# Normalising the softmax weights while they are split into halves, with four places for the halves, in a hybrid RG-LRU / forgetting-attention trunk on Trainium2

## The chip, the core and the metric

The kernel runs on one core of a Trainium2 chip. The metric is device time in microseconds (us) of one execution. A core has five engines that work side by side and meet through semaphores: PE multiplies matrices, DVE (VectorE) and ACT (ScalarE) do elementwise work and reductions, POOL (GpSimd) does slower elementwise work and issues some DMAs, and SP issues the rest of the DMAs. Every engine takes its instructions strictly in its own order: an instruction that waits holds back all that stand behind it on that engine.

## The reference, cut to what matters

Two layers: an RG-LRU layer, then forgetting attention (FoX) with 16 heads of 64 over 1024 positions, then a final norm. The change lies in the attention layer.

```python
def fox_mixer(h, w_in, b_f, w_out):
    u = h @ w_in
    q, k, v, gate = ...                       # (1, 1024, 16, 64) each, gate (1, 1024, 1024)
    cum = jnp.cumsum(jax.nn.log_sigmoid(f_logit), axis=1)
    ...
    logits = jnp.einsum("bqhd,bkhd->bhqk", q_blk, kf) * scale
    logits = logits + (cq_blk[..., :, None] - ck[:, :, None, :])
    logits = jnp.where(mask[None, None], logits, NEG_INF)
    p = jax.nn.softmax(logits, axis=-1)
    o = jnp.einsum("bhqk,bkhd->bqhd", p, vf)
    ...
    y = o * jax.nn.silu(gate)
    return y @ w_out
```

## The kernel before

Float32 products are made of halves: an operand is split into a high part and a low part (`to_hi`, `to_lo`, lines 88 to 102), and three products of parts are summed. The first 440 us hold the RG-LRU layer, which the change leaves as it is. The attention layer follows.

**One block of softmax** (`maxima`, line 718). A head's 1024 queries are taken in 8 blocks of 128 (i = 0 to 7); block i has (i+1)·128 keys. For each block: PE makes the logits S in PSUM (two places for S); DVE adds the mask and takes the row's maximum m in one custom instruction (line 742); ACT takes the exponential p and the row's sum (line 747); ACT writes the high half of p, times a constant, as float16 (line 752, booked on line 93); DVE writes the low half (line 753); one DMA issued by SP turns both halves over (`pT`, line 754), since the next product needs the keys on the partitions. There are two places for p, and two for the pair of halves, called `pp`. A place of `pp` is free again when its transposing DMA has landed. Below, "high half" and "low half" mean the two instructions that fill `pp`.

**The weighted values** (`weigh`, line 784). PE multiplies v with `pT` into O (PSUM) for half a head's queries, c = 0 (blocks 0 to 3) or c = 1 (blocks 4 to 7). ACT copies one part of O to `yo`, DVE adds the other (lines 804 and 805).

**The row sums.** Softmax divides by them. At the end of a head the 8 sums are scaled and inverted on DVE (lines 763 and 764), turned by PE (`tr`, line 766), copied (`rc`), written to DRAM and read back as a broadcast over 64 partitions by two DMAs on POOL's queue (`recd`, `recb`, lines 769 and 773). POOL multiplies the gate `sg` by them (`scale`, line 782), and then `yo` by the gate (`gated`, line 814). For heads up to 12 `yo` then goes to DRAM (`y1d`, line 820).

**The values of four heads** (`values`, line 541, and `bound`, line 524). Heads 0, 4, 8 and 12 begin with new v. 192 products `vps` make 8 tiles of 128 positions, 24 products each. Four tiles have room in PSUM: the 97th product needs the first tile to be read out. The read-out needs a factor: ACT squares the 8 weight tiles (`sqw`, two places), PE sums each over its rows (`norms`), DVE takes the maximum, ACT a square root, DVE a reciprocal and the factors `rv`; then ACT and DVE read the tiles out (lines 583 and 584).

**The order.** The text `ORDER` (line 29, and `LAST` for heads 12 to 15) says how PE's products are woven: a 0 or 1 is a step of `weigh` or `maxima`, a point is a step of six products of the projections around it (the next pair's q, k and gate; at the end the output product). From this a scheduler that simulates the engines fixes the order of every engine at build time. SP and POOL queues are in order as well; an issue on SP waits until the DMA eight issues earlier has landed. At the end, sums `xp` of the output are written to DRAM by POOL's queue (`x1d`, line 891) and read back by SP.

Of the kernel before, what the change touches and what calls it, by code (L numbers as in the profile page):

```python
# [23 lines left out]
NB = 12  # L24
HEADS = 16
HD = 64
# [14 lines left out]
def trunk(ctx: ExitStack, tc: tile.TileContext, xt, w0, wg, wo0, pc, gn, gf, w1, wv, wf, bf, wo1, out):  # L41
    nc = tc.nc

    def pool(name, bufs, **kw):
        return tc.tile_pool(name=name, bufs=bufs, **kw)

    const = ctx.enter_context(pool("const", 1))
    dram = ctx.enter_context(pool("dram", 1, space=DRAM))
    hpool = ctx.enter_context(pool("hT", 16))
    wpool = ctx.enter_context(pool("w", 4))  # L50
    ps = ctx.enter_context(pool("ps", 2, space=PSUM))
# [12 lines left out]
    ident = const.tile([P, P], F32, name="ident")  # L64
# [16 lines left out]

    pct = const.tile([P, 8, NB], F32, name="pct")
    gnt = const.tile([P, 2, KT], F32, name="gnt")
    cw = [pct[:, j] for j in range(4)]
    cb, ba, bx, ap_ = (pct[:, j] for j in range(4, 8))

# [102 lines left out]
    with ExitStack() as l0:  # L189
        xpool = l0.enter_context(pool("x", 1))  # L190
        ypool = l0.enter_context(pool("y", 2 * GROUP))
        lru = l0.enter_context(ExitStack())
# [9 lines left out]

        sm = const
        c2 = sm.tile([P, NB], F32, name="c2")
# [290 lines left out]
    cumd = dram.tile([HEADS, 2, SEQ], F32, name="cumd")  # L495
    recd = dram.tile([HEADS, 8, P], F32, name="recd")

    with ExitStack() as l1:
# [25 lines left out]
        def bound(g, parts):  # L524

            row = ps.tile([P, HALF], F32, tag="O", name="norms")[:, :256]
            for k in range(KT):
                sq = at.tile([P, 256], BF16, tag="sqw", name="sqw", bufs=2)
                nc.scalar.activation(sq, f32(parts[k][0][:, :256]), AF.Square, scale=gnt[:, 1, k : k + 1])
# [3 lines left out]
            nc.scalar.activation(most, most, AF.Sqrt, bias=tiny, scale=SEQ / TOP / TOP)  # L533
            nc.vector.reciprocal(most, most)
# [56 lines left out]
        sgs = {}  # L591
        recs = {}
        yos = {}
# [55 lines left out]

        fz = const.tile([P, 8, HEADS], F32, name="fz")  # L650
        Vs = {}
        bft = const.tile([HEADS, 1], F32, name="bft")
        nc.sync.dma_start(bft, bf)
        unit = at.tile([HEADS, HALF], F32, tag="recb", name="unit", bufs=1)
        nc.gpsimd.memset(unit, 1.0)
        cum = at.tile([HEADS, SEQ], F32, tag="sg", name="cum")

        def forget(half):
            cs = slice(half * HALF, (half + 1) * HALF)
            pt = ps.tile([P, HALF], F32, tag="O", name="fps")  # L660
            for i in range(4):
                if half and i > 1:
                    yield
                with tc.issue_after(pe[0].ins):
                    transpose(pt[:HEADS, i * P : (i + 1) * P], fz[:, half * 4 + i], ident)
            z_, e_ = (at.tile([HEADS, HALF], F32, tag=t, name=n, bufs=2) for t, n in (("p", "z"), ("pp", "e")))
            parts = [at.tile([HEADS, HALF], F32R, tag="yo", name="cp", bufs=2) for i in (3, 4)]
# [50 lines left out]
        def maxima(hd, c):  # L718
# [7 lines left out]
            for i in range(4 * c, 4 * c + 4):  # L726
# [26 lines left out]
                nc.vector.scalar_tensor_tensor(both[:, :, 1], p, TOP, both[:, :, 0], ALU.mult, ALU.subtract)  # L753
                nc.sync.dma_start_transpose(
# [3 lines left out]
                yield  # L758
            if hd == HEADS - 1 or c == 1:
                b0, b1 = (4 * c if hd == HEADS - 1 else 0), 4 * c + 4  # L760
                nb = b1 - b0
                sums = sums[:, b0:b1]
                nc.vector.tensor_scalar(sums, sums, tops[hd // 4], 2.0 * TOP, ALU.mult, ALU.mult)
                nc.vector.reciprocal(sums, sums)
                tr = ps.tile([P, P], F32, tag="O", name="tr")
                nc.tensor.transpose(tr[:nb], sums, ident)
                rc = at.tile([8, P], F32, tag="rc", name="rc", bufs=1)
                nc.vector.tensor_copy(rc[:nb], tr[:nb])
                nc.gpsimd.dma_start(recd[hd, b0:b1], rc[:nb])
                if s == 0:  # L770
                    recs[pair] = at.tile([P, SEQ], F32, tag="recb", name="recb", bufs=1)
                rows = slice(s * HD, (s + 1) * HD)
                nc.gpsimd.dma_start(
                    recs[pair][rows, b0 * P : b1 * P],
                    recd[hd : hd + 1, b0:b1].rearrange("o b q -> o (b q)").to_broadcast([HD, nb * P]),
                )
                yield

        def scale(hd, cs=slice(0, SEQ)):
            rows = slice((hd % 2) * HD, (hd % 2 + 1) * HD)  # L780
            sg = sgs[hd // 2][rows, cs]
            nc.gpsimd.tensor_tensor(sg, sg, recs[hd // 2][rows, cs], ALU.mult)

        def weigh(hd, c, sub=slice(0, HALF)):
# [18 lines left out]
            r0, r1 = s * HD, (1 - s) * HD  # L803
            nc.scalar.copy(yo[r0 : r0 + HD], O[r1 : r1 + HD])
            nc.vector.tensor_tensor(yo[r0 : r0 + HD], yo[r0 : r0 + HD], O[r0 : r0 + HD], ALU.add)
            yield

        def gated(hd, c, sub=slice(0, HALF)):

            if hd % 2 == 0:  # L810
                return
            pair = hd // 2
            yo = yos[pair, c][:, sub]
            nc.gpsimd.tensor_tensor(
                yo, yo, sgs[pair][:, c * HALF + sub.start : c * HALF + sub.stop], ALU.mult
            )
            if hd == 15:
                split_y(c, pair, yo, sub)
            elif hd < 13:
                nc.sync.dma_start(y1d[c, pair], yo)  # L820
# [90 lines left out]
        def turned(c, q):  # L911
# [11 lines left out]
            for b in range(2):  # L923
# [4 lines left out]
                for h, (d0, nd) in enumerate(parts):  # L928
# [6 lines left out]
                    for k in range(2):  # L935
# [5 lines left out]
                        if k == 0:  # L941
                            yield
                    sq = at.tile([P, HALF], F32, tag="pp", name="sq1", bufs=2)[:, : nd * P]
                    nc.scalar.activation(sq, pt, AF.Square, accum_out=ss[:, min(h, ss.shape[1] - 1)].unsqueeze(1))
# [59 lines left out]
        for hd in range(HEADS):  # L1004
# [28 lines left out]
            scale(hd)  # L1033
            gated(hd, 0)
# [17 lines left out]
        quarters = [slice(0, 256), slice(256, HALF)]  # L1052
        scale(15, slice(0, HALF))
# [4 lines left out]
        scale(15, slice(HALF, SEQ))  # L1058
        gated(15, 1, quarters[0])
# [76 lines left out]
```

## Time and profile before

| what | value |
|---|---|
| time, median of 3 runs | 1126.28 us (1125.81 to 1129.25) |
| the profiled execution's own time | 1126.19 us |
| its span, first to last instruction | 1124.4 us |
| PE busy | 1067.5 us (95% of the span) |
| DVE, ACT, POOL busy | 760.9, 611.2, 195.1 us |
| mean granted PE clock | 0.989 of full |

The profiled execution agrees with the median to 0.1 us, so its rows can be used for the sum directly. In the page's rows a time is in us, a group shows its count, busy time and mean duration in ns, and "idle before" is the time for which the engine stood still ahead of an instruction, with what ended it. A row of waits reads: engine, tile and line that waited, what it waited for, total us, number, longest. In rows by stage the columns are from:to, length, busy us of PE, of PE's weight loads, of DVE, ACT and POOL (with counts), granted PE clock, DMA share and GB/s.

### The profile page before, as it was taken

To read this page: it belongs to the slowest core of one execution; us is meant where nothing else is said; L and a number is where in the kernel's file an instruction comes from. 1 tells how busy PE (TensorE), PEld (TensorE's weight loads), DVE (VectorE), ACT (ScalarE), POOL (GpSimd) and SP (SyncE) were. 2 spreads that over 40 slices of the span, in tenths; PEclk is the share of its full clock that TensorE was granted. 3 is DMA by queue.
4 is the path that set the end of the run, shared out by engine and by line. 5 is a ranking of instruction groups with operands and counts; after the bars stand their busy time and mean duration, and the time that the engine had idled before them with its cause. 6 is when DMAs were issued, how large, how long until landed. Compare 5 with 4: busy or idle time off the path is not lost.

```text
span 1124.4 us, 14773 instructions
## 1 busy us (share of the span) xinstructions
PE 1067.5 (95%) x5147; PEld 850.3 (76%) x5147; DVE 760.9 (68%) x1216; ACT 611.2 (54%) x1053; POOL 195.1 (17%) x155
## 2 busy tenths in 40 slices
PE   9999999999999999899998999998999999989987
PEld 7788888888888887787666787667866678767666
DVE  7888755776568789547766557675567655677645
ACT  8488345355453656456555555565555555454434
POOL 1322212221121201420121201212012120112220
PEclk9999999999999999989998999999999999999999
DMA  6111111111111114417898938997398982999795
GB/s 236 57 47 43 52 52 52 38 58 45 53 38 52 47 44 144 130 56 164 176 192 161 181 81 177 192 181 177 87 177 185 164 179 73 227 229 220 195 244 187
DMA packets 214450, 143.13 MB, mean 127 GB/s; under 512 B 161348, under 2 KB 176324, under 8 KB 214376
## 3 DMA queue, kind: packets, MB, share of 16 engines
q1 hardware_dynamic: 211256, 133.73, 50.6%
q0 software_dynamic: 3120, 8.46, 2.6%
q8 instruction: 41, 0.67, 0.3%
q14 instruction: 33, 0.27, 0.1%
HBM read 63.30 MB, written 15.93 MB: 70 GB/s over the span
## 4 chain that ended last, share of the span: by engine, by line
PE 63%; DMA 17%; DVE 10%; ACT 5%; issue 3%; SPq 1%; POOL 0%; ACTq 0%; DVEq 0%; POOLq 0%
PE gps L56 19%; PE ops L56 13%; DMA pT<-pp 13%; PE ups L56 12%; PE vps L56 8%; PE gate L56 3%; DVE pp L753 3%; PE turn L56 3%; PE O L56 2%; ACT pp L93 2%; DVE S L742 2%; PE S L56 2%; DMA wf<-in_wo 1%; ACT p L747 1%; DVE wl L102 1%
## 5 line engine op out<-in xcount | busy, mean ns | idle before, releaser
L56 PE MATMUL gps<-hh,wh 128*128 128x512 f32 x576 | 234.9, 408 | 0.7 <-DVE qkl L621 0.7
L56 PE MATMUL gps<-hl,wh 128*128 128x512 f32 x576 | 228.2, 396 | 0.0
L56 PE MATMUL gps<-hh,wl 128*128 128x512 f32 x576 | 227.5, 395 | 0.0
L753 DVE SCALAR_TENSOR_TENSOR pp<-p,pp 128x128 f16<-128x128 f32 (+7 forms) x128 | 111.1, 868 | 118.4 <-ACT pp L93 117.5
L102 POOL TENSOR_TENSOR wl<-wf,wh 128x512 fp32r<-128x512 f32 (+1 forms) x60 | 100.8, 1685 | 397.5 <-ACT wh L91 359.9
L91 ACT CAST wh<-wf 128x512 fp32r<-128x512 f32 (+2 forms) x156 | 93.5, 603 | 112.3 <-PE ops L56 47.8
L93 ACT ACTIVATE pp<-p 128x128 f16<-128x128 f32 (+7 forms) x128 | 87.4, 684 | 113.8 <-DMA pT<-pp 112.4
L56 PEld LDWEIGHTS gps<-hl,wh 128*128 128x128 f32 x576 | 109.0, 189 | 25.9 <-issue 0.5
L56 PEld LDWEIGHTS gps<-hh,wh 128*128 128x128 f32 x576 | 109.6, 190 | 23.9 <-DVE qkl L621 0.9
L56 PE MATMUL S<-T,U 96*128 96x512 f32 (+7 forms) x384 | 98.7, 367 | 28.1 <-ACT p L747 28.1
L56 PEld LDWEIGHTS gps<-hh,wl 128*128 128x128 f32 x576 | 109.6, 190 | 20.1
L747 ACT ACTIVATE p<-S,m 128x128 f32<-128x128 f32 (+7 forms) x128 | 94.3, 737 | 51.1 <-DVE m L742 49.6
L56 PEld LDWEIGHTS S<-T,U 128*128 128x128 f32 (+1 forms) x384 | 68.5, 195 | 51.3 <-ACT p L747 39.4
L742 DVE CUSTOM_DVE_ANT_0 S<-S,mask 128x128 f32<-128x128 f32 (+7 forms) x128 | 96.6, 757 | 8.7 <-PE S L56 7.0
L387 DVE TENSOR_TENSOR x<-x,ops 128x512 f32<-128x512 f32 x80 | 54.1, 682 | 47.6 <-PE ops L56 47.6
L56 PE MATMUL O<-pT,v 128*128 128x512 f16 (+3 forms) x396 | 77.8, 324 | 4.0 <-DMA pT<-pp 1.8
L56 PE MATMUL vps<-wh,hh 128*128 128x256 f32 (+1 forms) x256 | 74.5, 291 | 7.3 <-DVE v L584 4.0
L102 DVE TENSOR_TENSOR wl<-wf,wh 128x512 fp32r<-128x512 f32 x96 | 68.1, 712 | 16.6 <-ACT wh L91 16.4
L56 PE MATMUL ups<-hh,wh 128*128 128x512 f32 x192 | 76.2, 398 | 0.9 <-ACT hh L93 0.9
L56 PE MATMUL ups<-hl,wh 128*128 128x512 f32 x192 | 76.6, 399 | 0.0
L56 PE MATMUL ops<-yh,wh 128*128 128x512 f32 x192 | 76.0, 396 | 0.5 <-DVE x L480 0.5
L56 PE MATMUL ups<-hh,wl 128*128 128x512 f32 x192 | 76.3, 397 | 0.0
(190 smaller groups left out, 2043.5 us busy)
## 6 DMA issues: line engine op xcount, KB each, us to landing
wf<-in_w SPq DMA_DIRECT2D x100, 256.0 KB
wf<-in_wo SPq DMA_DIRECT2D x64, 128.0 KB
U<-qkh SPq DMA_DIRECT2D x64, 128.0 KB
T<-qkh SPq DMA_DIRECT2D x28, 256.0 KB
x<-in_xt SPq DMA_DIRECT2D x16, 256.0 KB
x1d<-x SPq DMA_DIRECT2D x16, 256.0 KB
wf<-in_wv SPq DMA_DIRECT2D x16, 256.0 KB
U<-qkl SPq DMA_DIRECT2D x32, 128.0 KB
```

The source lines that it names most:

```text
L56: pe[0] = nc.tensor.matmul(*args, **kw)
L91: nc.scalar.copy(hi, src)
L93: nc.scalar.activation(hi, src, AF.Copy, scale=scale)
L102: return eng.tensor_tensor(lo, src, f32(hi), ALU.subtract)
L387: nc.vector.tensor_tensor(x, x, pt, ALU.add)
L742: nc.vector.tensor_tensor_reduce(S[:, :n], S[:, :n], mask[:, SEQ - n :], -1.0, -NEG, ALU.add, ALU.min, accum_out=m)
L747: seen[0] = nc.scalar.activation(p, S[:, :n], AF.Exp, bias=m, scale=-1.0, accum_out=sums[:, i : i + 1])
L753: nc.vector.scalar_tensor_tensor(both[:, :, 1], p, TOP, both[:, :, 0], ALU.mult, ALU.subtract)
```

## The change

- The row sum r of a block is divided by `TOP` on POOL (one number for each of 128 rows) and inverted on DVE, straight after the exponential. The high and the low half take r as their scale, in place of the constant. So each block's weights leave already normalised.
- The sums' path at the end of a head goes: DVE's scaling and inversion, the PE transposition `tr`, the copy `rc`, the DMAs `recd` and `recb`, and POOL's `scale`.
- `pp` has four places instead of two.
- The factor that undoes the scale of v, which the sums had carried, is now one number for four heads (`unit`). It is applied where O is read out: ACT's copy and DVE's addition take it as a scale.
- `gated` moves from POOL to DVE.
- To make room in SBUF, some tiles share places: `sqw` takes the two places of `yo`, `fz` and the tile of ones take those of `pT`, and some constants go into a pool that ends with the first layer.

```diff
-                sq = at.tile([P, 256], BF16, tag="sqw", name="sqw", bufs=2)
+                sq = at.tile([P, 256], BF16, tag="yo", name="sqw", bufs=2)
...
             nc.scalar.activation(most, most, AF.Sqrt, bias=tiny, scale=SEQ / TOP / TOP)
+            unit_ = tops[g] = const.tile([P, 1], F32, name=f"unit{g}")
+            nc.vector.tensor_scalar(unit_, most, 0.5 / TOP, None, ALU.mult)
             nc.vector.reciprocal(most, most)
-            tops[g] = most
...
-                both = at.tile([P, 8, 2, P], FP16, tag="pp", name="pp", bufs=2)[:, : i + 1]
+                both = at.tile([P, 8, 2, P], FP16, tag="pp", name="pp", bufs=4)[:, : i + 1]
                 p = p.rearrange("p (j k) -> p j k", k=P)
-                to_hi(both[:, :, 0], p, nc.scalar, scale=TOP)
-                nc.vector.scalar_tensor_tensor(both[:, :, 1], p, TOP, both[:, :, 0], ALU.mult, ALU.subtract)
+                r = sums[:, i : i + 1]
+                nc.gpsimd.tensor_scalar(r, r, 1.0 / TOP, None, ALU.mult)
+                nc.vector.reciprocal(r, r)
+                to_hi(both[:, :, 0], p, nc.scalar, scale=r)
+                nc.vector.scalar_tensor_tensor(both[:, :, 1], p, r, both[:, :, 0], ALU.mult, ALU.subtract)
...
-            if hd == HEADS - 1 or c == 1:
-                b0, b1 = (4 * c if hd == HEADS - 1 else 0), 4 * c + 4
-                ...
-                nc.vector.tensor_scalar(sums, sums, tops[hd // 4], 2.0 * TOP, ALU.mult, ALU.mult)
-                nc.vector.reciprocal(sums, sums)
-                tr = ps.tile([P, P], F32, tag="O", name="tr")
-                nc.tensor.transpose(tr[:nb], sums, ident)
-                ...
-                nc.gpsimd.dma_start(recd[hd, b0:b1], rc[:nb])
-                ...
-        def scale(hd, cs=slice(0, SEQ)):
-            ...
-            nc.gpsimd.tensor_tensor(sg, sg, recs[hd // 2][rows, cs], ALU.mult)
...
-            nc.scalar.copy(yo[r0 : r0 + HD], O[r1 : r1 + HD])
-            nc.vector.tensor_tensor(yo[r0 : r0 + HD], yo[r0 : r0 + HD], O[r0 : r0 + HD], ALU.add)
+            to, one = yo[r0 : r0 + HD], tops[hd // 4]
+            nc.scalar.activation(to, O[r1 : r1 + HD], AF.Copy, scale=one[r1 : r1 + HD])
+            nc.vector.scalar_tensor_tensor(to, O[r0 : r0 + HD], one[r0 : r0 + HD], to, ALU.mult, ALU.add)
...
-            nc.gpsimd.tensor_tensor(
+            nc.vector.tensor_tensor(
                 yo, yo, sgs[pair][:, c * HALF + sub.start : c * HALF + sub.stop], ALU.mult
             )
```

The order changes at three places that matter below.

The first is ACT's order in the wide blocks of one head. `p,sums` is the exponential, `pp` the high half, `wh` a weight's high part. Before:

```order
L747 ACTIVATE p,sums<-S,m 128x640 [waits DVE_49]
L93 ACTIVATE pp<-p 128x5x128 [waits DMAHW3_49,Activation_49]
L747 ACTIVATE p,sums<-S,m 128x768 [waits DVE_49]
L91 CAST wh<-wf 128x512 [waits PE_49]
L93 ACTIVATE pp<-p 128x6x128 [waits DMAHW7_49,Activation_49]
L747 ACTIVATE p,sums<-S,m 128x896 [waits DVE_49]
```

and now:

```order
L746 ACTIVATE p,sums<-S,m 128x640 [waits DVE_49,Activation_49]
L746 ACTIVATE p,sums<-S,m 128x768 [waits DVE_49,Activation_49]
L90 ACTIVATE pp<-p,sums 128x5x128 [waits DMAHW1_49,DVE_49,Activation_49]
L88 CAST wh<-wf 128x512 [waits PE_49]
L90 ACTIVATE pp<-p,sums 128x6x128 [waits DMAHW2_49,DVE_49,Activation_49]
L746 ACTIVATE p,sums<-S,m 128x896 [waits DVE_49,PE_49]
```

The next block's exponential now stands ahead of a block's high half, which waits for DVE's reciprocal.

The second place is PE's order in the values of four heads (the second such group, at 636 to 660 us before). `sqw` are the squared weights, `norms` their sums. The last of the eight `norms`, before, with what follows it:

```order
L56 LDWEIGHTS onesb
L56 MATMUL norms<-sqw,onesb 128x256 [waits Activation_49]
L56 MATMUL vps<-wl,hh 128x256
L56 MATMUL vps<-wh,hh 128x256
L56 MATMUL vps<-wh,hl 128x256
```

and now the last three:

```order
L56 MATMUL norms<-sqw,onesb 128x256 [waits Activation_49]
L56 MATMUL vps<-wl,hh 128x256
L56 LDWEIGHTS onesb
L56 MATMUL norms<-sqw,onesb 128x256 [waits Activation_49]
L56 LDWEIGHTS onesb
L56 MATMUL norms<-sqw,onesb 128x256 [waits Activation_49]
L56 MATMUL vps<-wh,hh 128x256 [waits DVE_49,PE_49]
```

Of the 96 products that have room in PSUM, 80 stood ahead of the last `norms` and 16 behind it; now all 96 stand ahead. The fourth `sqw` waits on ACT for the DMA that writes `yo` to DRAM, whose place it takes (`sqw<-wh,gnt 128x256 [waits DMAHW1_49,DVE_49]`). It is the same in all three later groups; the first group is as before. Apart from this, from one transposition of the forget gates, and from the removed `tr`, PE's order is the same.

The third place is POOL's queue in heads 12 to 15. It held the sums' DMAs and scalings between the stores of `xp`; now it holds one-column scalings of sums:

```order
L891 DMA x1d<-xp 128x512 [waits DMAHW4_49,DVE_49]
L891 DMA x1d<-xp 128x512 [waits DMAHW5_49,DVE_49]
L814 TENSOR_TENSOR yo<-yo,sg_8535 128x512 [waits DVE_49,Pool_49]
L891 DMA x1d<-xp 128x512 [waits DMAHW0_49,DMASW6_49,DVE_49]
L769 DMA recd<-rc 4x128 [waits DMASW7_49,DVE_49]
L773 DMA recb<-recd 64x512 [waits DMASW7_49,DMASW0_49]
L891 DMA x1d<-xp 128x512 [waits DMAHW3_49,DMASW1_49,DVE_49]
```

and now:

```order
L752 TENSOR_SCALAR sums<-sums 128x1 [waits Activation_49] x2
L869 DMA x1d<-xp 128x512 [waits DMAHW5_49,DMASW1_49,DVE_49]
L752 TENSOR_SCALAR sums<-sums 128x1 [waits Activation_49]
L869 DMA x1d<-xp 128x512 [waits DMAHW4_49,DMASW2_49,DVE_49]
L869 DMA x1d<-xp 128x512 [waits DMAHW0_49,DMASW3_49,DVE_49]
L752 TENSOR_SCALAR sums<-sums 128x1 [waits Activation_49]
```

The stores no longer stand behind the broadcast's DMAs; some row sums stand behind stores.

More of the change, by code (lines that the diff above doesn't have):

```diff
@@ L190, in trunk @@
         xpool = l0.enter_context(pool("x", 1))
+        pct = xpool.tile([P, 8, NB], F32, name="pct")
+        cw = [pct[:, j] for j in range(4)]
+        cb, ba, bx, ap_ = (pct[:, j] for j in range(4, 8))
         ypool = l0.enter_context(pool("y", 2 * GROUP))
@@ L200, in long @@
             return tmp.tile([P, SEQ], dtype, tag=tag, name=tag, bufs=bufs)
-        sm = const
+        sm = xpool
         c2 = sm.tile([P, NB], F32, name="c2")
@@ L647, in trunk @@
         drain(kq_units(0, ((1, (0,)), (0, (0,)))))
-        fz = const.tile([P, 8, HEADS], F32, name="fz")
+        fz = at.tile([P, 8, HEADS], F32, tag="pT0", name="fz", bufs=1)
         Vs = {}
@@ L653, in trunk @@
         nc.sync.dma_start(bft, bf)
-        unit = at.tile([HEADS, HALF], F32, tag="recb", name="unit", bufs=1)
+        unit = at.tile([HEADS, HALF], F32, tag="pT1", name="unit", bufs=1)
         nc.gpsimd.memset(unit, 1.0)
@@ L665, in forget @@
                     transpose(pt[:HEADS, i * P : (i + 1) * P], fz[:, half * 4 + i], ident)
-            z_, e_ = (at.tile([HEADS, HALF], F32, tag=t, name=n, bufs=2) for t, n in (("p", "z"), ("pp", "e")))
+            z_, e_ = (at.tile([HEADS, HALF], F32, tag=t, name=n, bufs=b) for t, n, b in (("p", "z", 2), ("pp", "e", 4)))
             parts = [at.tile([HEADS, HALF], F32R, tag="yo", name="cp", bufs=2) for i in (3, 4)]
@@ L942, in turned @@
                             yield
-                    sq = at.tile([P, HALF], F32, tag="pp", name="sq1", bufs=2)[:, : nd * P]
+                    sq = at.tile([P, HALF], F32, tag="pp", name="sq1", bufs=4)[:, : nd * P]
                     nc.scalar.activation(sq, pt, AF.Square, accum_out=ss[:, min(h, ss.shape[1] - 1)].unsqueeze(1))
```

22 lines of the change are left out of this document (removed).

## The prediction

> **What bounds the kernel now.** I read the page's busy times first, then the waits of the whole core and of PE alone, then single stages.
>
> ```profile
> span 1124.4 us, 14773 instructions
> PE 1067.5 (95%) x5147; PEld 850.3 (76%) x5147; DVE 760.9 (68%) x1216; ACT 611.2 (54%) x1053; POOL 195.1 (17%) x155
> ```
>
> PE works 95% of the span, so this is a PE kernel: time can come only from PE's own work, from its 56.9 us of idleness, and from a lowered clock. The page's mean granted clock, 0.989, stands for some 12 us (0.011 of 1124.4). Whose waits matter, the list of waits tells (engine, tile and line that waited, releaser: total us, times, longest):
>
> ```profile
> DVE pp L753 <- ACT pp L93: 117.5, 75, 7.1
> ACT pp L93 <- DMA pT<-pp: 112.4, 71, 6.2
> POOL sg L782 <- DMA recb<-recd: 75.0, 17, 6.9
> POOL x1d L891 <- DVE xp L890: 53.5, 11, 25.1
> ...
> PE S L56 <- ACT p L747: 28.1, 22, 2.9
> ...
> PE vps L56 <- DVE v L584: 4.0, 3, 1.3
> ```
>
> ACT stands 112.4 us before the high half, because both places of the halves are still being turned over by DMAs; DVE's low half passes this on. Of all that, only the row of S reaches PE: PE waits 28.1 us for an exponential to free S. That is half of PE's idleness. How the one leads to the other shows at 600 to 611 us, in the order of time on ACT, DVE and PE:
>
> ```profile
> 606.65 0.63 ACT L93 ACTIVATE pp<-p 128x512 f16<-128x512 f32 x1 [5.97 <-DMA pT<-pp]
> ```
>
> ```profile
> 607.32 1.62 DVE L753 SCALAR_TENSOR_TENSOR pp<-p,pp 128x512 f16<-128x512 f32 x1 [6.86 <-ACT pp L93]
> 608.86 0.69 DVE L521 TENSOR_TENSOR gps<-gps,rs 128x512 f32<-128x512 f32 x1
> 609.46 0.82 DVE L742 CUSTOM_DVE_ANT_0 S<-S,mask 128x640 f32<-128x640 f32 x1
> ```
>
> ```profile
> 611.30 1.86 PE L56 MATMUL S<-T,U 128*128 128x512 f32 x4 [2.89 <-ACT p L747]
> ```
>
> The high half comes 5.97 us late, the low half after it, and the next block's mask stands behind the low half on DVE. Two blocks on, PE stands 2.89 us. The stages right behind show a second price (from:to, length, busy us of five engines, clock, DMA share, GB/s):
>
> ```profile
> 608.00:611.00 3.00, 0.41 (x2) 0.00 (x0) 3.00 (x6) 1.23 (x2) 0.38 (x1) 0.97 0.45 105
> 611.00:614.00 3.00, 2.69 (x7) 2.31 (x8) 2.88 (x5) 2.55 (x7) 0.00 (x0) 0.50 0.77 161
> 614.00:617.00 3.00, 3.00 (x9) 2.32 (x8) 1.77 (x4) 2.86 (x6) 0.00 (x0) 0.50 0.80 165
> ...
> 890.00:895.00 5.00, 5.00 (x17) 3.98 (x16) 4.35 (x8) 4.43 (x10) 0.00 (x0) 0.66 0.77 166
> ```
>
> After the stall the clock is halved for 6 us, which costs 6 × 0.50 = 3 us more. A stall near 889 us leaves 0.66 over 5 us, 1.7 us. I count 6 us in all for this behind the waits for S.
>
> [...]
>
> **The change, part by part.**
>
> *Four places for the halves.* ACT's wait for the DMA goes where the fourth-last transposition has landed instead of the second-last. In the wide blocks the next exponential also stands ahead of the high half now, so S is freed before any such wait. Bounds: nothing (the DMA is the limit, below) to all of 28.1 us and the 6 us of clock. I take 22 of the 28.1, leaving 6 for heads 12 to 15, where DVE itself is full, and 6 us of clock: −28.
>
> *Later transpositions.* What is late next is `pT`, if the DMA can't keep up. Now it hardly is:
>
> ```profile
> PE O L56 <- DMA pT<-pp: 1.8, 3, 0.8
> ```
>
> ```profile
> 720.00:760.00 40.00, 36.75 (x172) 26.90 (x171) 28.71 (x56) 24.41 (x48) 4.79 (x4) 1.00 0.93 191
> ```
>
> ```profile
> 625.45 3.04 SPq L754 DMA_TRANSPOSE pT<-pp  x1
> ```
>
> ```profile
> 604.08 0.84 PE L56 MATMUL S<-T,U 128*128 128x320 f32 x4
> ...
> 630.65 1.02 PE L56 MATMUL O<-pT,v 128*128 128x512 f16 x4 [0.73 <-issue]
> ```
>
> ```profile
> 630.64 0.42 ACT L93 ACTIVATE pp<-p 128x256 f16<-128x256 f32 x1 [2.07 <-DMA pT<-pp]
> ```
>
> The widest block (128 x 16 x 128 in float16, 512 KB) is issued at 625.45 and its place is free at 630.6: 5.2 us. The four wide blocks are 26/8 of that, 17 us if one ran at a time. From the S of the first of them to the weighted values that need the last (both rows of PE) are 26.6 us, 20.7 without the stall of 2.9 and its clock, and the first low half is ready some 5 us into them: S 1.0, mask 0.8, then the exponential, high half and low half at about 0.8 each, and signals. So it is near. Bounds: 0 to 1.2 us in each of 15 heads, 18 us; I take +4, since two transpositions overlap and the broadcast's DMAs go.
>
> *The row's scale in the chain.* For each of 128 blocks, POOL and DVE do one column. The nearest rows:
>
> ```profile
> L1118 POOL MEMSET const-float32-1.0<- 128x1 f32 x1 | 0.1, 108 | 0.0
> ```
>
> ```profile
> L753 DVE SCALAR_TENSOR_TENSOR pp<-p,pp 128x512 f16<-128x512 f32 x16 | 25.2, 1572 | 55.4 <-ACT pp L93 55.4
> ...
> L753 DVE SCALAR_TENSOR_TENSOR pp<-p,pp 128x640 f16<-128x640 f32 x16 | 13.3, 832 | 6.8 <-ACT pp L93 6.8
> ...
> L763 DVE TENSOR_SCALAR sums<-sums,most 128x8 f32<-128x8 f32 x15 | 3.4, 227 | 0.0
> L764 DVE RECIPROCAL sums<-sums 128x8 f32<-128x8 f32 x15 | 3.0, 198 | 0.3
> ...
> L534 DVE RECIPROCAL most<-most 128x1 f32<-128x1 f32 x4 | 0.7, 164 | 1.5 <-ACT most L533 1.5
> ```
>
> DVE gains 128 × 0.164 = 21 us of work, and 12 us of `gated` (17 at about 0.7, the row of `gps` above), but loses the sums' 17 × (0.23 + 0.20) = 7 us and their copies. The low half of 512 columns takes 1572 ns against 832 for 640 columns; the one at 607.32 ran beside POOL's `scale`, which goes. That is some 16 × 0.85 = 14 us back. DVE's total stays near 68%. On ACT the high half waits POOL's 0.11, DVE's 0.16 and what stands ahead on DVE, and the next exponential (about 1 us in a wide block) covers it. I cost it at nothing in heads 0 to 11, and +2 us in heads 12 to 15, where row sums stand on POOL behind stores that wait for DVE (53.5 us in the row of `x1d`, 25.1 of them before the first store). If the cover is gone it is the fourth rival.
>
> *The removed transpositions* `tr`: 17 on PE.
>
> ```profile
> 564.70 0.08 PEld L766 LDWEIGHTS tr<-ident,sums 128*8 128x8 f32 x1
> 564.92 0.27 PE L766 MATMUL tr<-ident,sums 128*8 128x128 f32 x1
> ```
>
> Between 0.08 and 0.35 us each, 0.2 taken: −3. POOL's 75 us of waiting for the broadcast go too, and are worth nothing: no wait of PE names them.
>
> *The squares in the places of `yo`.* Now PE idles 1.3 us per group of values (the row `PE vps` above: 4.0 in 3):
>
> ```profile
> 646.62 0.28 PE L56 MATMUL norms<-sqw,onesb 128*128 128x256 bf16 x1
> ...
> 648.52 0.28 PE L56 MATMUL vps<-wl,hh 128*128 128x256 f32 x1
> 650.13 0.36 PE L56 MATMUL vps<-wh,hh 128*128 128x256 f32 x1 [1.32 <-DVE v L584]
> ```
>
> ```profile
> L529 ACT ACTIVATE sqw<-wh,gnt x32: 492/508/512, 462.7 to 921.1; 128x256 bf16<-128x256 f32 x32
> ```
>
> From the end of the last norm (646.90) to the next product it takes 3.23 us: maximum, root, reciprocal, factors, read-out. 16 products cover 1.9 of it. In the new order nothing covers it, one small instruction (`unit`, 0.23 by the row of `sums`) joins it, and the last square can start only when the sixth norm is done: 0.51 of its own, 0.28 of the norm, some 0.3 of signals, 1.1 together. So 1.1 + 3.5 less the 0.2 of two norms: 4.4 us idle, 3.1 more than now. The fourth square also waits for `yo`'s store. `x1d<-xp`, of the same 256 KB, takes 4.1 us to land:
>
> ```profile
> x1d<-xp POOLq DMA_DIRECT2D x16, 256.0 KB, 4.1
> ...
> 642.78 0.54 SPq L820 DMA_DIRECT2D y1d<-yo  x1
> ```
>
> Today's issue at 642.78 would land at 646.9, 1.4 us after PE reaches the fourth norm's new place (25 products of 1.9/16 = 0.119 before 648.52: 645.5). But the store will be issued earlier: its chain on ACT and DVE loses some 3 us of waiting for `pp` and the slow low half, and `gated` no longer waits for POOL. I take no delay here, with 0 to 3 us as bounds. Idleness of 4.4 us is longer than the 2.89 that halved the clock, so 3 us follow, as there. 3 groups × (3.1 + 3) = +18. Bounds: 3 × 2.5 = 8 without the clock, to 3 × 9 = 27.
>
> [...]
>
> *The end.* PE waits for sums that POOL stores late:
>
> ```profile
> 1076.96 1.28 POOL L814 TENSOR_TENSOR yo<-yo,sg 128x512 f32<-128x512 f32 x1 [4.01 <-DMA xp<-x1d]
> ...
> 1084.69 1.46 PE L56 MATMUL turn<-ident,x 128*128 128x128 f32 x4 [2.59 <-DMA x<-x1d]
> ```
>
> The stores stand behind the broadcast on POOL's queue, which goes. Of the 2.59 and a clock of 0.66 over the next 4 us (1.4), 4 in all, I take −3.
>
> Sum: −22 − 6 + 4 + 2 − 3 + 18 − 3 = −10; 1126.2 − 10 = 1116 us. The profiled execution (1126.19) and the median (1126.28) are the same for this purpose.
>
> **The rivals.**
>
> *All of it works* (1104). The squares' idleness costs no clock (−9) and the last waits for S go in part (−3). For it: shorter idleness leaves the clock alone, as in a stage in which PE idles 1.9 us of 5:
>
> ```profile
> 990.00:995.00 5.00, 3.10 (x15) 1.91 (x14) 5.00 (x10) 3.72 (x6) 0.00 (x0) 1.00 1.01 257
> ```
>
> Against: 4.4 us in one piece is well beyond 2.89.
>
> *The DMA is the limit, not its places* (1129). With a DMA share of 0.93 before, waits for S turn into waits for `pT`: 1.2 us in 15 heads, 18 in place of 4, so 1116 + 14 = 1130, less 1 where they overlap. For it: the 17 us of transpositions worked out above in some 15. Against: the share falls to half in the stages with values, and second halves of heads carry 10 units where the first carry 26. It decides once the last wide block lands later than 21 us after the first one's S.
>
> *Nothing gained* (1126): the places' gain and the squares' loss cancel, with the rest near zero. The change then does do what it says, but PE doesn't see it.
>
> *The scale's chain is exposed* (1137, slower). ACT's order is fixed: where DVE's reciprocal stands behind an operation of 0.7 to 1.2 us, the high half waits, then the low half, and the exponential two blocks on, which needs the place of p. If 0.3 to 1 us of each of the 32 wide pairs reaches PE, that is 10 to 32 us, 21 in the middle: 1116 + 21. For it: DVE is full for whole wide bursts (3.00 of 3.00 at 608 to 611). Against: the next exponential stands between, and S is freed earlier. It decides where the high half's mean wait for DVE passes some 1 us.
>
> **How the numbers follow.** Forecast 1116 (its own range 1107 to 1123): 0.46. All works: 0.15. DMA limit: 0.20. Nothing gained: 0.04. Exposed chain: 0.15. Runs differ by 0.3% (3.4 us), which is about what a measurement here can tell. Faster: 0.45 of the forecast, all of the first rival, 0.02 of the second: 0.62. Same: 0.01, 0.04 and 0.02 of the DMA's case: 0.07. Slower: 0.31. The range goes from 1101 to 1134: it leaves out half the first rival's lower side and most of the exposed chain's upper half, 0.16 together.
>
> **What would show it.** Right: ACT's wait for `pT<-pp` falls from 112 us to below 40 and PE's wait for S from 28 to some 6; PE's wait for v rises from 4 to 12 or more in three places, each followed by a clock near 0.5; no `tr`, `recd` or `recb`; `turn` waits less. Wrong: PE waits for `pT` of over 10 us (the DMA), waits of ACT's high half for DVE of over 60 us with waits for S as before (the chain), or a wait for v below 2 us each.

## The result, and the profile after

The changed kernel takes 1134.24 us (median of 9 runs, 1130.11 to 1140.27), the kernel before beside it 1127.43. The ratio is 1.0061, with a 95% interval of 1.0036 to 1.0087: slower by 0.6%, where 1116 us and faster were forecast. The profiled execution of the changed kernel is the longest of its nine, 1140.27 us, so its rows overstate the loss by 6 us. They are used for where time goes; how much a part is worth is taken from the experiments.

The page of the changed kernel, its span and busy times:

```profile
span 1138.5 us, 14931 instructions
PE 1074.5 (94%) x5130; PEld 857.5 (75%) x5130; DVE 761.8 (67%) x1314; ACT 624.9 (55%) x1053; POOL 151.9 (13%) x215
```

PE idles 64.0 us (1138.5 − 1074.5; before 56.9), and its work takes 7.0 us longer with 17 products fewer. The mean granted clock is 0.975 (before 0.989). Of the changed kernel's list of waits, the rows that matter here:

```profile
PE O L56 <- DMA pT<-pp: 21.5, 10, 3.6
...
PEld L56 <- DMA pT<-pp: 15.4, 5, 4.0
ACT sqw L528 <- DMA y1d<-yo: 13.7, 6, 5.2
PE vps L56 <- DVE v L584: 11.7, 3, 3.9
...
ACT pp L90 <- DVE sums L753: 9.1, 12, 2.6
...
PE ops L56 <- ACT wh L88: 5.5, 1, 5.5
PE turn L56 <- DMA x<-x1d: 4.5, 1, 4.5
...
PE S L56 <- ACT p L746: 3.7, 4, 1.7
...
ACT pp L90 <- DMA pT<-pp: 2.6, 4, 1.1
```

The change does what it says. ACT's wait for a place of the halves is down from 112.4 to 2.6 us, and PE's wait for S from 28.1 to 3.7. In its place PE waits 21.5 us for the transposed weights `pT` (1.8 before), in ten stalls of up to 3.6 us. (The row PEld is the weight load ahead of such a product, which waits for the same transfer.) The wait for v has tripled, as forecast. Late in the program come one wait of 5.5 us at `ops`, the products of the output, and one of 4.5 us at `turn`, the transpositions of the last stage (2.6 before).

One such stall in the order of time, and the stages behind it (columns as in the tables by stage before):

```profile
569.03 1.04 PE L56 MATMUL O<-pT,v 128*128 128x512 f16 x4 [3.56 <-DMA pT<-pp]
```

```profile
569.00:572.00 3.00, 2.96 (x10) 2.09 (x10) 0.75 (x1) 0.72 (x1) 0.00 (x0) 0.66 0.78 190
572.00:575.00 3.00, 3.00 (x13) 1.43 (x12) 0.00 (x0) 0.00 (x0) 0.00 (x0) 0.77 0.66 130
```

After 3.56 us of idleness the clock stands at 0.66 and 0.77 for two stages of 3 us, which costs another 1.7 us (3 × 0.34 + 3 × 0.23).

Two landmarks show in which part of the program the time was lost: the last start of `norms` (the fourth group of values) and the first product that writes `turn` from `woh` (the last stage, just behind its wait). Of the kernel before:

```profile
L56 PE MATMUL norms<-sqw,onesb x32: 269/282/285, 468.3 to 923.9; 128*128 128x256 bf16 x32
...
L56 PE MATMUL turn<-woh,yhh x34: 278/397/776, 1085.8 to 1117.9; 128*128 128x512 f32 x30, 128*128 128x256 f32 x4
```

and of the changed kernel:

```profile
L56 PE MATMUL norms<-sqw,onesb x32: 269/283/287, 469.8 to 930.1; 128*128 128x256 bf16 x32
...
L56 PE MATMUL turn<-woh,yhh x34: 276/398/776, 1099.5 to 1131.9; 128*128 128x512 f32 x30, 128*128 128x256 f32 x4
```

Up to the fourth group 6.2 us are lost (930.1 − 923.9), from there to the last stage 7.5 more (169.4 in place of 161.9), and in the last stage itself hardly anything (39.0 to the last instruction, in place of 38.6). The wait at `ops` (5.5), the clock behind it (2.5, below) and the longer wait at `turn` (1.9) are enough for the 7.5.

### The profile page after: what moved, and what is told of

It reads as the page before. It is cut to its first block, busy times and chain, and to the rows that moved or that the text cites. A ratio compares the mean times of both kernels' runs of the same rounds, so it can differ in the third digit from the quotient of the medians.

```text
span 1138.5 us, 14931 instructions
## 1 busy us (share of the span) xinstructions
PE 1074.5 (94%) x5130; PEld 857.5 (75%) x5130; DVE 761.8 (67%) x1314; ACT 624.9 (55%) x1053; POOL 151.9 (13%) x215
## 5 line engine op out<-in xcount | busy, mean ns | idle before, releaser
L755 DVE SCALAR_TENSOR_TENSOR pp<-p,sums,pp 128x128 f16<-128x128 f32 (+7 forms) x128 | 104.1, 814 | 28.1 <-ACT pp L90 27.2
L90 ACT ACTIVATE pp<-p,sums 128x128 f16<-128x128 f32 (+7 forms) x128 | 97.9, 771 | 27.2 <-DVE sums L753 9.1
L752 POOL TENSOR_SCALAR sums<-sums 128x1 f32<-128x1 f32 x128 | 37.8, 295 | 497.2 <-ACT p L746 497.1
L56 PE MATMUL O<-pT,v 128*128 128x512 f16 (+3 forms) x396 | 83.2, 340 | 21.5 <-DMA pT<-pp 21.5
L56 PE MATMUL S<-T,U 96*128 96x512 f32 (+7 forms) x384 | 93.7, 353 | 3.7 <-ACT p L746 3.7
L56 PE MATMUL vps<-wh,hh 128*128 128x256 f32 (+1 forms) x256 | 76.9, 301 | 15.3 <-DVE v L584 11.7
L56 PEld LDWEIGHTS <-v 128*128 128x128 f16 x396 | 33.2, 102 | 68.9 <-issue 37.4
```

Of the source, the lines that this page charges most:

```text
L56: pe[0] = nc.tensor.matmul(*args, **kw)
L90: nc.scalar.activation(hi, src, AF.Copy, scale=scale)
L752: nc.gpsimd.tensor_scalar(r, r, 1.0 / TOP, None, ALU.mult)
L755: nc.vector.scalar_tensor_tensor(both[:, :, 1], p, r, both[:, :, 0], ALU.mult, ALU.subtract)
```

## The experiments

Two theories stood against each other. By the first, the transpositions are issued late, since a block's halves now wait for its row's scale (the chain ACT, POOL, DVE, ACT). By the second, the DMA can't turn the halves over faster, so the waits would only change their name. Beside them stood the squares in the places of `yo`. All twelve results, with the ratio to the kernel before on the same chip:

| kernel | median us | ratio to before (95%) |
|---|---|---|
| changed kernel | 1134.24 | 1.0061 (1.0036 to 1.0087) |
| e_order: projections ahead of the weighted values | 1112.56 | 0.9851 (0.9815 to 0.9888) |
| e_const: halves don't wait for the scale | 1112.09 | 0.9850 (0.9822 to 0.9879) |
| e_notop: no POOL step in the chain | 1118.72 | 0.9905 (0.9880 to 0.9930) |
| e_dve: that step on DVE | 1147.65 | 1.0174 (1.0153 to 1.0195) |
| e_hop3: one DVE step more | 1153.80 | 1.0226 (1.0202 to 1.0251) |
| e_sqwp: squares in the places of p | 1122.79 | 0.9946 (0.9922 to 0.9970) |
| e_pp2: two places for the halves | 1150.89 | 1.0193 (1.0162 to 1.0223) |
| b_order: kernel before, order of e_order | 1127.20 | 0.9985 (0.9970 to 1.0001) |
| e_both: e_order and e_sqwp | 1106.39 | 0.9791 (0.9766 to 0.9817) |
| e_all: e_both and e_notop | 1092.58 | 0.9683 (0.9661 to 0.9704) |
| e_alld: e_both and e_dve | 1113.83 | 0.9854 (0.9828 to 0.9880) |
| e_allpp2: e_all with two places | 1129.01 | 0.9997 (0.9981 to 1.0013) |

### More cover ahead of the weighted values

```diff
-ORDER = "1.1.1.1..0.0", "1.1.1.1.0.00.0"
+ORDER = "1.1.1.1..0.0", "1.1.1.1...0000"
```

> The changed kernel with another order text for a head's second half: two steps of projections (six products each, some 1.4 us each) stand ahead of the weighted values that need the last transposed blocks, instead of behind their first step. If the transpositions are only late (issued some 3 us later because the halves wait for the row's scale and stand behind the next exponential), 2.7 us of cover takes most of the 3.6 us stalls away: PE's waits for pT (O, 21.5 us in 10; weights, 15.4 in 5) fall below 10 together, the clock in the stretches from 560 to 960 us goes back to about 0.98, and the time falls to 1120 to 1126. If the DMA's throughput is the limit, the transpositions of the next head start later by as much, the waits for pT stay above 15 us in O, and the time is 1130 to 1136.

It took 1112.56 us, 21.7 less than the changed kernel. From PE's waits in it:

```profile
PE vps L56 <- DVE v L584: 10.2, 3, 3.4
PE S L56 <- ACT p L746: 6.6, 7, 2.2
PE turn L56 <- DMA x<-x1d: 5.9, 2, 5.4
...
PE O L56 <- DMA pT<-pp: 3.6, 6, 1.5
```

The wait for `pT` fell from 21.5 to 3.6 us, by moving twelve products in the second half of each head (heads 0 to 11). The DMA moved the same bytes in less time (194 GB/s from 560 to 600 us, in place of 178), so its throughput was not what set the changed kernel's time. The gain is larger than forecast. The stalls' 18 us alone would not make it; the clock behind them comes back too (1.00 from 560 to 600 us in place of 0.96, 0.984 in the mean in place of 0.975).

### The halves without the scale

```diff
-                to_hi(both[:, :, 0], p, nc.scalar, scale=r)
-                nc.vector.scalar_tensor_tensor(both[:, :, 1], p, r, both[:, :, 0], ALU.mult, ALU.subtract)
+                to_hi(both[:, :, 0], p, nc.scalar, scale=TOP)
+                nc.vector.scalar_tensor_tensor(both[:, :, 1], p, TOP, both[:, :, 0], ALU.mult, ALU.subtract)
```

> The changed kernel with the halves scaled by the constant TOP again instead of the row's scale r. POOL's division and DVE's reciprocal are still made, but no half waits for them; the weights are left unnormalised. This takes the dependence alone out of the chain. If the chain row sum, POOL, DVE, high half is what makes the transpositions late: DVE's reciprocals no longer stand between, PE's waits for pT fall from 21.5 (O) and 15.4 (weights) to below 8 together, and the time falls by those waits and their clock, to 1112 to 1120. If the DMA's throughput is the limit, the waits for pT stay above 25 us together and the time within 4 us of 1134, since the transpositions have the same sizes.

1112.09 us. This kernel leaves out the normalisation, so it serves for the price alone. The scale is still worked out on POOL and DVE; only nobody waits for it. So the row's scale in the halves costs 22 us. Nearly all of that has to be the waiting, but not quite: with a constant the instructions themselves are shorter too (for 640 columns the high half takes 737 ns in place of 822, the low half 811 in place of 877), and no run prices this by itself. The next experiment keeps the longer halves. PE's waits for `pT` fell to 8.7 us in O and 8.5 in weight loads, above the 8 together that I had named: a part is left that isn't the chain's. The first wide transposition that both kernels issue in the same head tells the size. In the changed kernel, the product S of the second wide block on PE, and the transposition's issue on SP:

```profile
547.84 0.87 PE L56 MATMUL S<-T,U 128*128 128x512 f32 x4
```

```profile
553.60 1.66 SPq L756 DMA_TRANSPOSE pT<-pp  x1
```

and in this one:

```profile
546.93 0.87 PE L56 MATMUL S<-T,U 128*128 128x512 f32 x4
...
565.87 1.04 PE L56 MATMUL O<-pT,v 128*128 128x512 f16 x4 [1.30 <-DMA pT<-pp]
```

```profile
549.66 1.36 SPq L756 DMA_TRANSPOSE pT<-pp  x1
```

From that S to the issue it takes 5.76 us (553.60 − 547.84) with the chain and 2.73 without. The weighted values can begin 21.2 us after it (569.03) with the chain, 18.9 without, and PE comes to them after 17.6 in both.

### One step fewer, one moved, one more

Without the division by `TOP`, so that the weights are normalised to 1:

```diff
-                nc.gpsimd.tensor_scalar(r, r, 1.0 / TOP, None, ALU.mult)
                 nc.vector.reciprocal(r, r)
```

(and `unit` without its `/ TOP`).

> The changed kernel with a shorter chain to the halves: POOL's division of the row sum by TOP is left out, DVE inverts the sum itself, and the constant goes from the factor unit, so that the weights are normalised to 1 in place of TOP (the halves are less exact for it). One hop of four (ACT, POOL, DVE, ACT) goes, 0.2 us of work and two signals. If the length of the chain decides when the transpositions are issued, the waits for pT fall by a third or more (21.5 + 15.4 to below 25 us) and the time is 1122 to 1130. If what counts is only that the high half stands behind the next exponential (the order), or the DMA's throughput, it stays within 4 us of 1134.

1118.72 us, 15.5 less than the changed kernel and better than expected. The step's own busy time is 0.3 us per block on an engine that had little to do:

```profile
L752 POOL TENSOR_SCALAR sums<-sums 128x1 f32<-128x1 f32 x128 | 37.8, 295 | 497.2 <-ACT p L746 497.1
```

With the same division on DVE:

```diff
-                nc.gpsimd.tensor_scalar(r, r, 1.0 / TOP, None, ALU.mult)
+                nc.vector.tensor_scalar(r, r, 1.0 / TOP, None, ALU.mult)
```

> The changed kernel with the division by TOP moved from POOL to DVE, right ahead of the reciprocal there: the same numbers, one engine fewer in the chain, 128 more instructions of some 0.2 us on DVE. Changed kernel 1134, without the division 1118.7. If it is the hop over POOL (its signals, its queue) that costs, this comes out at 1118 to 1124: the hop goes, DVE's 0.2 us per block stays. If it is the work of the step itself, wherever it is done, or if fuller DVE delays masks and low halves as much as the hop did, 1129 to 1136.

1147.65 us: outside both ranges, and 13 us slower than with the hop over POOL. With one DVE step more:

```diff
+                nc.vector.tensor_scalar(r, r, 2.0, None, ALU.mult)
-                nc.gpsimd.tensor_scalar(r, r, 1.0 / TOP, None, ALU.mult)
+                nc.gpsimd.tensor_scalar(r, r, 0.5 / TOP, None, ALU.mult)
```

> The changed kernel with the suspected cost made larger: a DVE step (the row sum times 2) ahead of POOL's (times a half and by TOP), so that the chain to the halves is ACT, DVE, POOL, DVE, ACT; the numbers are the same. If the chain's length decides, one hop fewer having been worth 15.5 us, one hop more costs about as much: 1144 to 1154, with waits for pT in O and weights above 45 us together. If the removal of POOL's step helped for another reason (POOL's stores at the end, the scheduler's order), it stays within 5 us of 1134.

1153.80 us, in the range of the first theory, though the waits for `pT` (28.0 and 11.4 us) stayed below the 45 named.

So neither the hop's signals nor the step's 0.15 to 0.3 us of work is the price. What is, shows in one wide block (5 × 128 keys), on DVE, in the order of time. The changed kernel, where the row's sum is read at 548.32 to 548.51 and POOL's step runs at 548.59:

```profile
548.75 0.97 DVE L741 CUSTOM_DVE_ANT_0 S<-S,mask 128x768 f32<-128x768 f32 x1
...
549.63 0.16 DVE L753 RECIPROCAL sums<-sums 128x1 f32<-128x1 f32 x1
```

```profile
548.32 0.19 ACT L746 ACTIVATION_READ_ACCUMULATOR p<-S,m 128x1 f32 x1
549.87 0.90 ACT L746 ACTIVATE p<-S,m 128x768 f32<-128x768 f32 x1 [1.35 <-DVE sums L753]
...
550.76 0.82 ACT L90 ACTIVATE pp<-p,sums 128x640 f16<-128x640 f32 x1
```

The same block without the step:

```profile
547.94 0.19 ACT L746 ACTIVATION_READ_ACCUMULATOR p<-S,m 128x1 f32 x1
548.45 0.83 ACT L90 ACTIVATE pp<-p,sums 128x640 f16<-128x640 f32 x1 [0.32 <-DVE sums L752]
```

```profile
548.27 0.15 DVE L752 RECIPROCAL sums<-sums 128x1 f32<-128x1 f32 x1
548.37 0.97 DVE L741 CUSTOM_DVE_ANT_0 S<-S,mask 128x768 f32<-128x768 f32 x1
```

and with the step on DVE:

```profile
551.36 0.13 DVE L752 TENSOR_SCALAR sums<-sums 128x1 f32<-128x1 f32 x1
551.46 0.97 DVE L741 CUSTOM_DVE_ANT_0 S<-S,mask 128x768 f32<-128x768 f32 x1
...
552.34 0.16 DVE L753 RECIPROCAL sums<-sums 128x1 f32<-128x1 f32 x1
```

Without the step the reciprocal stands ahead of the next block's mask, and the high half starts 0.3 us after the sum is read. With POOL's step the order has the reciprocal behind the mask (0.97 us), the next exponential ahead of the high half on ACT, and the high half starts 2.3 us after the sum (550.76 − 548.51). With two DVE steps the mask lies between them. (The 1.35 us for which ACT stands ahead of that exponential are a wait for the mask: it starts 0.15 us after the mask's end, and the row names the reciprocal only because that ended last.) In this block the price of a step in the chain is thus not its own duration but that of what stands ahead of it in DVE's and ACT's order. In ACT's order this can be counted over the whole program, as the number of blocks (of 128) whose high half stands behind a later block's exponential:

| kernel, same order text | high halves behind a later exponential | median us |
|---|---|---|
| kernel before | 9 | 1127.43 |
| e_const | 1 | 1112.09 |
| e_notop | 40 | 1118.72 |
| changed kernel | 54 | 1134.24 |
| e_dve | 59 | 1147.65 |
| e_hop3 | 71 | 1153.80 |

Among the five with four places the times go with the count. So does the lateness that the traces show: from the read sum to the start of the high half, averaged over the 64 wide blocks, it is 0.1 us in e_const, 1.4 in e_notop, 1.7 in the changed kernel, 1.9 in e_dve and 2.5 in e_hop3. That the count alone makes the time isn't shown; it is the sign of late halves that the order itself gives. Why the step costs 13 us more on DVE than on POOL, with only five more such blocks, stays open. e_order has the changed kernel's 54, since its edit moves only PE's products: it covers the lateness.

The wait at `ops` goes with the chain as well: 5.5 us in the changed kernel, 1.8 in e_const, and none for a weight's high part in e_notop. The last stage doesn't: from its first product with `woh` to the last instruction it takes 39.0 us in the changed kernel and 39.1 in both others.

### The squares

```diff
-                sq = at.tile([P, 256], BF16, tag="yo", name="sqw", bufs=2)
+                sq = at.tile([P, 256], BF16, tag="p", name="sqw", bufs=2)
```

> The changed kernel, with one part undone: the squares of the weights (sqw) no longer share the places of yo, they take the two places of p. Changed kernel 1134, before 1127. If sharing yo's places is what makes PE idle 3.9 us in three groups of values and lowers the clock there: PE's wait for v falls from 11.7 us in 3 to about 4 in 3, ACT's 13.7 us of waiting for the DMA that stores yo goes, and the time falls by 3 x 6 = 18 us less what is left of today's 1.3 us waits: 1118 to 1122. Rival: the squares now wait for a place of p instead (until the low half is written), the wait for v stays near 11 us, and the time stays within 4 us of 1134. PE's waits for pT (21.5 + 15.4 us) should stay by either theory.

1122.79 us, 11.4 less, near the upper end of the first range but outside it. ACT no longer waits for the store of `yo` (13.7 us in the changed kernel). The wait for v fell to 6.3 us in 3, and the waits for `pT` stayed (22.4 and 14.8), as both theories had it. In the second group of values PE's stall is now short, and the clock behind it stays whole:

```profile
646.02 0.36 PE L56 MATMUL vps<-wh,hh 128*128 128x256 f32 x1 [2.10 <-DVE v L584]
```

```profile
646.00:649.00 3.00, 2.98 (x25) 3.00 (x26) 0.65 (x3) 0.27 (x2) 0.00 (x0) 1.00 0.03 8
```

In the changed kernel the same stall, and the stage behind it:

```profile
649.03 0.55 PE L56 MATMUL vps<-wh,hh 128*128 128x256 f32 x1 [3.90 <-DVE v L584]
```

```profile
649.00:652.00 3.00, 2.97 (x14) 3.00 (x15) 0.66 (x3) 0.27 (x2) 0.00 (x0) 0.52 0.04 8
```

That is 1.8 us of idleness and 1.4 of clock (3 × 0.48). In the other two groups the changed kernel's PE works 3.4 and 4.4 us at a clock of 0.50 behind its stalls (791.84 to 795.25 and 931.79 to 938.61), 1.7 and 2.2 us lost, and e_sqwp's at 1.00 (over all of 760 to 800 and 920 to 960 us). Together that makes 5.4 us of idleness (11.7 − 6.3) and 5.3 of clock, 10.7 of the 11.4.

### The places, and the order in the kernel before

```diff
-                both = at.tile([P, 8, 2, P], FP16, tag="pp", name="pp", bufs=4)[:, : i + 1]
+                both = at.tile([P, 8, 2, P], FP16, tag="pp", name="pp", bufs=2)[:, : i + 1]
```

> The changed kernel with two places for the halves again, so the normalisation alone. If the four places are what took PE's waits for S (28.1 to 3.7 us): ACT's wait for the transposing DMA comes back to 100 us or more, PE's wait for S to 20 to 30 us, and PE's waits for pT fall back somewhat; time 1145 to 1155, since the high half's place and the late halves now cost together. If instead the new order (next exponential ahead of the high half) took the waits for S, these stay below 10 us and the time stays within 5 us of 1134.

(The other tiles that use these places get two as well.) 1150.89 us, 16.7 more than with four places. ACT waits 86.2 us for a place and PE 17.2 for S, both a little below the ranges. The four places do take the waits for S, and the change without them loses 2% (it still has the shared places of `sqw`).

The kernel before, with the order text of e_order:

> The kernel before (two places, weights not normalised, sums broadcast) with the same new order text. If the gain of the new order is the lateness of this change's transpositions, there is little to gain here: PE waited 1.8 us for pT, and holds S back 28 us for want of places of pp, which later weighted values don't mend; they hold pT longer, and the time is 1124 to 1134. If the old order was simply a worse one for both kernels, it gains about 20 us here too: 1105 to 1112.

1127.20 us, ratio 0.9985 (0.9970 to 1.0001): no gain that can be told from none. PE waits 28.3 us for S there, as without it. The new order mends what the change brought and is no better order in itself.

### Together

e_both has the edits of e_order and e_sqwp, e_all that of e_notop as well, e_alld that of e_dve in its place.

> The changed kernel with both edits: the order text with two projection steps ahead of the weighted values of a head's second half, and the squares in the places of p. The order alone gave 1112.6, the squares alone 1122.8, the changed kernel 1134.2. If the two losses lie in different places (waits for pT in the heads, waits for v in the three groups of values) they add: 1134.2 - 21.7 - 11.4 = 1101, between 1099 and 1105. Rival: the order's delay shifts the heads' work into the groups of values and the two share a loss: 1108 to 1112.

> All three edits on the changed kernel: new order text, squares in the places of p, no POOL step in the chain (weights normalised to 1). If the order has already covered the chain, the shorter chain adds little: within 4 us of the kernel with the two edits, 1097 to 1105. If the chain still costs in heads 12 to 15 and at the end, whose order text is unchanged, it gains 5 to 8 more: 1093 to 1097.

> The candidate with full exactness: new order text, squares in the places of p, division by TOP on DVE. With the same two edits, POOL's step gave 1106.4 and no step 1092.6. If the hop over POOL is the cost, 1093 to 1098; if the step's work on DVE weighs as much, 1102 to 1107.

e_both took 1106.39 us, between its two ranges: the gains add but for some 5 us. e_all took 1092.58, a ratio of 0.9683 (0.9661 to 0.9704), 13.8 less than e_both and 0.4 below the lowest range: the shorter chain pays where the order had already covered it. The step on DVE costs 7.4 us more than on POOL here too (1113.83), outside both ranges. In e_all PE waits for little (the first four of its list):

```profile
PE vps L56 <- DVE v L584: 5.7, 3, 1.9
PE turn L56 <- DMA x<-x1d: 4.3, 2, 3.7
PE vps L56 <- DVE fz L587: 3.5, 1, 3.5
PE O L56 <- DMA pT<-pp: 3.4, 3, 1.7
```

e_all is faster than both kernels by 3% and more. Its weights are normalised to 1 and not to `TOP`, which was expected to make the halves less exact (no run here measures it); e_both is the fastest with the change's own numbers.

Last, e_all with two places:

> The fastest kernel so far (new order text, squares in the places of p, no division by TOP; 1092.6) with two places for the halves again. In the changed kernel itself two places cost 16.7 us (1150.9 against 1134.2). If the four places are worth as much with the losses taken away, PE's waits for S come back to 17 us or more and the time is 1107 to 1115. If the normalisation's order alone (next exponential ahead of the high half) now frees S early enough, S waits stay below 10 us and the time is 1093 to 1100.

1129.01 us, as slow as the kernel before, and well beyond both ranges: with the losses taken away the four places are worth 36 us, more than twice what they are worth in the changed kernel. ACT waits 87.8 us for a place again and PE 23.5 for S:

```profile
DVE pp L754 <- ACT pp L90: 90.5, 72, 4.0
ACT pp L90 <- DMA pT<-pp: 87.8, 55, 4.4
```

Four places in the kernel before weren't tried, so what they are worth without the normalisation stays open.

## Why the prediction was wrong

- **The step that failed is "the row's scale in the chain".** It was costed at nothing in heads 0 to 11, because "the next exponential (about 1 us in a wide block) covers it". That exponential was not cover but part of the cost: it stands ahead of the high half because the half is late, and each late half delays its transposition. e_const prices the row's scale at 22 us. Two sizes were off too, both small against the 2 us by which the high half is late in the block above: POOL's step was taken at 0.11 us and takes 0.30, and each half takes some 0.07 to 0.09 us longer with a row's scale, for which the sum has no term. The longer halves can't explain the loss, since e_notop has them too and gains 15.5 us.
- **"Later transpositions, +4" was the same miss from its other side.** The prediction counted the cover from the first wide S to the last weighted values, and let the first low half be ready some 5 us into it, without asking what the chain adds. In the head above, the first transposition is issued 3.0 us later. PE's waits for `pT` came to 21.5 us and their clock. With 22 in place of 4 the prediction's own sum is 1134 (1116 + 18). That it meets the measured time is luck: the next terms were missed as well, and the experiments' prices don't simply add.
- **Four places, −22 and −6: right for the wait, too much for the time.** 24.4 us of the wait for S went. But e_pp2 prices the places at 16.7 us and not 28: with them PE's stalls moved to `pT` (10.0 us in O with two places, 21.5 with four), and the mean clock stayed low (0.977 with two, 0.975 with four).
- **The squares, +18: right in kind, too large.** Undoing them gave 11.4, and 2.3 us of additional wait for v are left in e_sqwp (6.3 against 4.0): some 14. The forecast for a group was 4.4 us of idleness and 3 of clock; the rows of the second group show 3.9 and, in the stage behind, 1.4.
- **The end, −3, and heads 12 to 15, +2: wrong sign, and too small.** The broadcast did leave POOL's queue, but the wait at `turn` rose from 2.6 to 4.5 us. Ahead of it, at 1051 to 1056.5 us, PE waits 5.5 us at `ops` for a weight's high part, and then works 5.0 us at half clock, 2.5 us more (the clock is at 0.50 from 1054.67 to 1061.49); the prediction has no such term. ACT stands 6.39 us before its cast for the load of that weight, and the load stands on SP behind two transpositions:

```profile
1043.89 7.93 SPq L756 DMA_TRANSPOSE pT<-pp  x2
1051.92 0.52 SPq L112 DMA_DIRECT2D wf<-in_wo  x1
```

- **The rivals.** "The scale's chain is exposed" (1137) named the cause and nearly the time, with a chance of 0.15, but the wrong way to PE (through S) and the wrong sign to look for: ACT's high half waits only 9.1 us for DVE in place of over 60, since the order of ACT was laid around the wait. "The DMA is the limit" (1130) named the sign that came true, waits for `pT` of over 10 us, but not the cause: e_order and e_const turn over the same blocks in 22 us less.

## What to carry to other kernels

Cost a new step in a chain of dependent instructions at what stands ahead of it on each engine it passes, not at its own duration. Where a scheduler lays out the order, look in that order for what now stands behind what: the wait itself hardly appears in the list of waits (9.1 us here, for a cost of 22), because other work was put into it. When a wait is removed, measure how far the next one on the same path is from binding, and move cover there in the same change: the four places were worth 36 us with the way behind them free, and 16.7 as they were built, which the rest of the change used up.

## What the runs showed of the hardware that was not expected

The sum of PE's stalls doesn't tell what they cost in clock. e_notop waits for `pT` in O nearly as long as the changed kernel (19.9 us against 21.5), in shorter pieces (13, the longest 2.3, against 10 of up to 3.6). Its mean clock is 0.992, against 0.975 in the changed kernel, which is worth some 19 us (0.017 of 1120). But the length of a single stall doesn't decide either. In the kernel before, a stall of 2.02 us was followed by half clock, and in e_notop one of 3.69 us (of the wait for v) was not:

```profile
859.87 0.72 PE L56 MATMUL S<-T,U 128*128 128x512 f32 x1 [2.02 <-ACT p L747]
```

```profile
856.56:859.96 3.40, 1.38 (x7) 0.81 (x5) 3.34 (x6) 1.60 (x4) 1.25 (x2) 1.00 0.64 160
859.97:863.38 3.41, 3.41 (x9) 2.84 (x10) 3.23 (x7) 2.66 (x5) 1.01 (x1) 0.50 0.84 220
863.40:866.80 3.40, 3.40 (x16) 2.75 (x16) 2.60 (x4) 0.76 (x2) 0.00 (x0) 1.00 1.11 252
```

```profile
779.23 0.36 PE L56 MATMUL vps<-wh,hh 128*128 128x256 f32 x1 [3.69 <-DVE v L584]
```

```profile
773.99:777.39 3.40, 1.55 (x13) 1.18 (x12) 1.10 (x5) 2.18 (x4) 0.00 (x0) 1.00 0.00 0
777.40:780.80 3.40, 1.57 (x13) 1.60 (x14) 2.16 (x8) 2.08 (x8) 0.00 (x0) 1.00 0.00 0
```

Behind the first stall the clock stands at 0.50 for a stage of 3.41 us and is back at 1.00 in the next; in e_notop it is at 1.00 in both stages that hold the second, and over the whole of 760 to 800 us. So between these two it was not the length that decided. What did is not shown here.
